# Four fp32 loads at the start of a Jensen-Shannon kernel, each split by partition halves over both hardware DMA queues, with p ahead of q

## The chip, the cores and the metric

The kernel runs on one core of one Trainium2 chip. The metric is device time in microseconds (us) of that core; lower is better. Times quoted are medians of several executions. Some executions fall in a slower state, over 1.5% above the fastest of the same kernel; they are called slow and the others fast. A ratio is the mean time of one kernel's fast runs over that of the other's of the same rounds, so it is not quite the ratio of the medians that stand beside it. The profiled execution has a *span* some 1.8 us shorter than its time, because the span leaves out what lies around the program.

## The reference

```python
batch, dim = 1024, 4096          # p and q: positive fp32 rows that sum to 1
m = 0.5 * (p + q)
kl_pm = np.sum(p * np.log(p / (m + 1e-8) + 1e-8), axis=-1)
kl_qm = np.sum(q * np.log(q / (m + 1e-8) + 1e-8), axis=-1)
return (0.5 * (kl_pm + kl_qm)).astype(np.float32)
```

## The kernel before

The rows lie eight to a partition, and the kernel walks through eight groups of 128 rows in blocks of columns. For each block it needs log p, log q and the log of the sum, all made by ScalarE (ACT). The first two blocks (512 and 256 columns, called block 0 and block 1 here) are loaded as fp32 by the hardware queues of SyncE (SP) and ScalarE. All others are loaded by GpSimd's queue, which casts to fp16 on the way; the third block (832 columns) is the first of these.

```python
for i in range(HW):                                   # HW = 2: blocks 0 and 1, fp32
    g, c0, w = loads[i]
    nc.sync.dma_start(out=early[i][:, 0, :], in_=pv[g, :, c0 : c0 + w])
    nc.scalar.dma_start(out=early[i][:, 1, :], in_=qv[g, :, c0 : c0 + w])
warm = small.tile([P, 1], fp32, tag="warm")
nc.vector.memset(warm, 1.0)
nc.scalar.activation(out=warm, in_=warm, func=Act.Ln)  # brings the table in
# ...
cast_loads(loads[HW : HW + 1])                        # third block, by GpSimd, with a cast
ident = small.tile([P, P], fp16, tag="ident")
make_identity(nc, ident)
# ...
cast_loads(loads[HW + 1 :])                           # all the rest
```

The order of work on ScalarE begins so (p, q: log of a block of p or q; c: log of a block's sum, which VectorE adds for blocks 0 and 1 and TensorE for all others):

```
p0 q0 c0 p1 q1 c1 p2 q2 c2 c3 p3 q3 c4 c5 ...
```

Of the kernel before, what the change touches and what calls it, by code (L numbers as in the profile page):

```python
# [91 lines left out]
def kernel(  # L92
# [6 lines left out]
    nc = tc.nc  # L99
    P = nc.NUM_PARTITIONS  # L100
# [13 lines left out]
    pv = p.rearrange("(p g) d -> g p d", g=n_rg)  # L114
    qv = q.rearrange("(p g) d -> g p d", g=n_rg)
# [35 lines left out]
    early = []  # L151
# [16 lines left out]

    for i in range(HW):
        g, c0, w = loads[i]  # L170
        nc.sync.dma_start(out=early[i][:, 0, :], in_=pv[g, :, c0 : c0 + w])
        nc.scalar.dma_start(out=early[i][:, 1, :], in_=qv[g, :, c0 : c0 + w])
    warm = small.tile([P, 1], fp32, tag="warm")
    nc.vector.memset(warm, 1.0)
    nc.scalar.activation(out=warm, in_=warm, func=Act.Ln)  # L175
    def cast_loads(some):
# [15 lines left out]
        out=half, in0=ident, scalar1=0.5, scalar2=0.0, op0=Alu.mult, op1=Alu.add  # L192
# [3 lines left out]
        out=less, in0=ident, scalar1=-0.5, scalar2=0.0, op0=Alu.mult, op1=Alu.add  # L196
# [242 lines left out]
    while any(queues):  # L439
        moved = False  # L440
        for todo in queues:
            while todo and all(d in emitted for d in after(*todo[0])):
                kind, i = todo.pop(0)
# [57 lines left out]
```

## Time and profile before

| | before |
|---|---|
| time, median of 6 runs | 98.19 us (97.82 to 98.51) |
| span of the profiled run | 96.0 us |
| ACT busy | 89.8 us, 94% of the span |
| ScalarE's first log, last log's end | 4.17 us, 92.25 us |

When each early load lands: the list of DMA issues of the kernel before, for the first 3.3 us, gives it. Its columns are: what is loaded, the queue that issues, count, size (for the casting loads in fp16), and us from the start of the issue to the landing.

```profile
t<-in_q_dram ACTq DMA_DIRECT2D x1, 256.0 KB, 3.6
t<-in_p_dram SPq DMA_DIRECT2D x1, 256.0 KB, 3.4
...
t<-in_p_dram POOLq DMA_DIRECT2D x1, 208.0 KB, 4.7
t<-in_q_dram POOLq DMA_DIRECT2D x1, 208.0 KB, 5.7
t<-in_q_dram ACTq DMA_DIRECT2D x1, 128.0 KB, 3.8
t<-in_p_dram SPq DMA_DIRECT2D x1, 128.0 KB, 3.4
```

With issues that start at 0.74 and 1.17 us, all four fp32 loads are there by 4.9 us. The casting loads of the third block are issued from 1.24 and 1.90 and land at 5.9 and 7.6.

### The profile page before, as it was taken

The numbers are of one execution on the slowest core, as the hardware profiler recorded it, in microseconds if no ns is written. First come the engines' busy times: TensorE is split into PE (matmuls) and PEld (weight loads), VectorE is DVE, ScalarE is ACT, GpSimd is POOL, SyncE is SP. The second block draws the span as 40 slices with busy tenths as digits, with TensorE's granted clock in tenths as the row PEclk, the third lists the DMA queues.
The fourth block names the chain that finished last, engine by engine and source line by source line (L and its number), as shares of the span: only waits on it lengthen the run. The fifth ranks groups of instructions, "written<-read, shape, count | busy, mean of one in ns | idle before, by whom it ended". The sixth has DMA issues, their size and how long they took to land.

```text
span 96.0 us, 1311 instructions
## 1 busy us (share of the span) xinstructions
PE 70.7 (74%) x468; PEld 45.3 (47%) x468; DVE 81.7 (85%) x87; ACT 89.8 (94%) x74; POOL 29.3 (31%) x60
## 2 busy tenths in 40 slices
PE   0799774886686678696785974984977989897740
PEld 0576441653465244463452642752552766656520
DVE  1378869999966988998979989979999999999990
ACT  3599999999999999999999999999999999999960
POOL 5974466443232424242313423335400000000000
PEclk9999999999999999999999999999999999999999
DMA  2999999999999999999999999999999999500000
GB/s 46 328 184 199 206 204 207 209 208 218 210 207 214 208 210 214 212 213 210 220 206 209 219 208 209 212 204 216 211 204 221 213 212 215 101 0 3 0 0 2
DMA packets 8502, 17.25 MB, mean 180 GB/s; under 512 B 1072, under 2 KB 3888, under 8 KB 8496
## 3 DMA queue, kind: packets, MB, share of 16 engines
q0 software_dynamic: 7776, 16.39, 90.1%
q1 hardware_dynamic: 432, 0.40, 1.5%
q10 hardware_dynamic: 288, 0.39, 1.2%
q8 instruction: 3, 0.05, 0.2%
q14 instruction: 3, 0.02, 0.1%
HBM read 33.55 MB, written 0.00 MB: 350 GB/s over the span
## 4 chain that ended last, share of the span: by engine, by line
ACT 43%; DMA 24%; issue 24%; DVE 2%; POOL 2%; PE 1%; ACTq 0%; POOLq 0%
ACT ab_t L281 25%; DMA t<-in_q_dram 24%; ACT c_t L299 17%; DVE c_t L343 1%; PE acc_t L360 1%; POOL t L179 1%; DVE ab_t L328 1%; POOL t L180 1%; ACT unused L371 0%; POOL ident masks.py:199 0%; POOL ident masks.py:197 0%; ACTq L299 0%; DVE res L376 0%; ACTq L496 0%; ACTq L281 0%
## 5 line engine op out<-in xcount | busy, mean ns | idle before, releaser
L281 ACT ACTIVATE ab_t<-t 128x2816 f16<-128x2816 f16 (+15 forms) x38 | 62.6, 1685 | 1.1 <-DMA t<-in_p_dram 1.0
L265 PE MATMUL st<-t,ident 128*128 128x512 f16 (+4 forms) x144 | 34.1, 352 | 7.4 <-DMA t<-in_q_dram 6.4
L311 DVE TENSOR_TENSOR ab_t<-ab_t,c_t 128x2816 f16<-128x2816 f16 (+12 forms) x25 | 29.3, 1180 | 6.7 <-ACT c_t L299 5.9
L360 PEld LDWEIGHTS <-half 128*128 128x128 f16 x268 | 25.4, 97 | 20.2 <-issue 16.3
L299 ACT ACTIVATE c_t<-st 128x1408 f16<-128x1408 f32 (+13 forms) x30 | 32.3, 1099 | 0.1
L360 PE MATMUL acc_t<-t,half 128*128 128x256 f16 (+2 forms) x200 | 23.9, 264 | 9.3 <-DVE t L321 9.0
L321 DVE TENSOR_TENSOR t<-t,ab_t 128x2816 f16<-128x2816 f16 (+11 forms) x23 | 28.2, 1234 | 1.2
L265 PEld LDWEIGHTS <-ident 128*128 128x128 f16 x144 | 13.6, 98 | 22.0 <-issue 11.7
L179 POOL DMA_DIRECT2D t<-in_p_dram x27 | 14.5, 536 | 20.4 <-DMA t<-in_p_dram 19.5
L180 POOL DMA_DIRECT2D t<-in_q_dram x27 | 14.4, 532 | 19.4 <-DMA t<-in_q_dram 19.3
L360 PE MATMUL acc_t<-ab_t,half 128*128 128x256 f16 x68 | 8.8, 270 | 2.4 <-DVE ab_t L328 2.4
L328 DVE TENSOR_TENSOR ab_t<-t,ab_t 128x1536 f16<-128x1536 f16 (+5 forms) x8 | 9.3, 1172 | 0.1
L253 PE MATMUL acc_t<-ones,ident 128*128 128x256 f16 x22 | 4.9, 420 | 3.1 <-POOL ident masks.py:199 3.1
L253 PEld LDWEIGHTS <-ident 128*128 128x128 f16 x22 | 3.2, 148 | 4.3 <-POOL ident masks.py:199 3.1
L339 DVE TENSOR_TENSOR c_t<-st,c_t 128x256 f16<-128x256 f32 (+2 forms) x3 | 3.7, 1217 | 0.0
L343 DVE CUSTOM_DVE_ANT_0 c_t<-st,c_t,run 128x1408 f16<-128x1408 f32 (+1 forms) x2 | 3.1, 1548 | 0.0
L343 DVE CUSTOM_DVE_ANT_0 c_t<-st,c_t 128x1024 f16<-128x1024 f32 (+1 forms) x2 | 3.0, 1484 | 0.0
L253 PE MATMUL acc_t<-ones,zero 128*128 128x256 f16 x22 | 2.9, 272 | 0.0
L175 ACT ACT_TABLE_LOAD x1 | 1.3, 1283 | 1.7 <-PEq L485 1.7
L382 DVE TENSOR_REDUCE res<-acc_t 128x1 f32<-128x256 f32 x6 | 2.5, 417 | 0.0
L253 PEld LDWEIGHTS <-zero 128*128 128x128 f16 x22 | 2.1, 98 | 0.2
L321 DVE TENSOR_TENSOR ab_t<-t,ab_t 128x1024 f16<-128x1024 f32 (+1 forms) x2 | 1.9, 958 | 0.1
(24 smaller groups left out, 9.7 us busy)
## 6 DMA issues: line engine op xcount, KB each, us to landing
t<-in_p_dram POOLq DMA_DIRECT2D x5, 352.0 KB, 12.4
t<-in_q_dram POOLq DMA_DIRECT2D x5, 352.0 KB, 12.8
t<-in_p_dram POOLq DMA_DIRECT2D x4, 384.0 KB, 11.8
t<-in_q_dram POOLq DMA_DIRECT2D x4, 384.0 KB, 12.0
t<-in_p_dram POOLq DMA_DIRECT2D x4, 320.0 KB, 12.7
t<-in_q_dram POOLq DMA_DIRECT2D x4, 320.0 KB, 12.8
t<-in_p_dram POOLq DMA_DIRECT2D x2, 512.0 KB, 13.3
t<-in_q_dram POOLq DMA_DIRECT2D x2, 512.0 KB, 14.5
```

Of the source, the lines that this page charges most:

```text
L179: nc.gpsimd.dma_start(out=v[:, 0, :], in_=pv[g, :, c0 : c0 + w])
L180: nc.gpsimd.dma_start(out=v[:, 1, :], in_=qv[g, :, c0 : c0 + w])
L253: nc.tensor.matmul(out=acc[g][:, :AW], lhsT=weights, rhs=ones, start=alone, stop=alone)
L265: nc.tensor.matmul(out=st[:, b : b + m], lhsT=ident, rhs=v[:, t, b : b + m], start=t == 0, stop=t == 1,)
L281: nc.scalar.activation(out=ab[k][:, which, o : o + w], in_=pq(g, c0, w)[:, which, :], func=Act.Ln, bias=TINY, scale=SHIFT,)
L299: nc.scalar.activation(out=c_t[:, :w], in_=s[j], func=Act.Ln, bias=SHIFT * 1e-8, scale=SHIFT * 0.5)
L311: nc.vector.tensor_tensor(out=v, in0=v, in1=c[j].unsqueeze(1).to_broadcast([P, 2, parts[j][2]]), op=Alu.subtract,)
L321: nc.vector.tensor_tensor(out=into, in0=u, in1=v, op=Alu.mult)
L328: nc.vector.tensor_tensor(out=ab[k], in0=u, in1=ab[k], op=Alu.mult)
L339: nc.vector.tensor_tensor(out=c[j], in0=s[j], in1=c[j], op=Alu.mult)
L343: nc.vector.tensor_tensor_reduce(out=c[j], in0=s[j], in1=c[j], scale=-0.5, scalar=before, op0=Alu.mult, op1=Alu.add, accum_out=now,)
L360: nc.tensor.matmul(out=acc[g][:, :m], lhsT=less if kind == "S" else half, rhs=v[:, t, b : b + m], start=(kind, i) == adds[g][0] and n == 0 ...
```

## The change

ScalarE waits 1.01 us for the first block of p. The change lets both queues fetch p first, half of the partitions each, and q after it, so that p is there sooner.

```diff
     for i in range(HW):
         g, c0, w = loads[i]
-        nc.sync.dma_start(out=early[i][:, 0, :], in_=pv[g, :, c0 : c0 + w])
-        nc.scalar.dma_start(out=early[i][:, 1, :], in_=qv[g, :, c0 : c0 + w])
+
+        for t, v in ((0, pv), (1, qv)):
+            for h, queue in ((0, nc.sync), (P // 2, nc.scalar)):
+                queue.dma_start(
+                    out=early[i][h : h + P // 2, t, :], in_=v[g, h : h + P // 2, c0 : c0 + w]
+                )
```

## The prediction

> **What bounds the kernel now.** I read the page first: the share of each engine, then the row of slices for ScalarE (ACT) and for the DMA engines.
>
> ```profile
> PE 70.7 (74%) x468; PEld 45.3 (47%) x468; DVE 81.7 (85%) x87; ACT 89.8 (94%) x74; POOL 29.3 (31%) x60
> ...
> ACT  3599999999999999999999999999999999999960
> ...
> DMA  2999999999999999999999999999999999500000
> ```
>
> Two things are near their limit together. ACT has 89.8 us of work in a span of 96.0 us, and the DMA engines are full from the second slice (2.4 us each) to the 34th, about 82 us. The change touches only the opening, so the question is what the opening is worth. The timeline of ACT shows it (start, duration, what, and in brackets the idle time before it):
>
> ```profile
> 0.74 0.89 ACTq L172 DMA_DIRECT2D t<-in_q_dram  x2
> 1.65 1.28 ACT L175 ACT_TABLE_LOAD   x1 [1.65 <-PEq L485]
> 2.95 0.20 ACT L175 ACTIVATE warm<-warm 128x1 f32<-128x1 f32 x1
> 4.17 1.15 ACT L281 ACTIVATE ab_t<-t 128x512 f16<-128x512 f32 x2 [1.01 <-DMA t<-in_p_dram]
> 5.22 0.61 ACT L299 ACTIVATE c_t<-s 128x512 f16<-128x512 f32 x1
> 5.74 0.71 ACT L281 ACTIVATE ab_t<-t 128x256 f16<-128x256 f32 x2
> 6.35 0.40 ACT L299 ACTIVATE c_t<-s 128x256 f16<-128x256 f32 x1
> 6.66 1.82 ACT L281 ACTIVATE ab_t<-t 128x832 f16<-128x832 f16 x2
> 8.58 0.93 ACT L299 ACTIVATE c_t<-st 128x448 f16<-128x448 f32 x2
> ```
>
> The second queue's two issues stand ahead of the table load, the table is ready at 3.15, and ACT then sits 1.01 us until the first block of p lands. That second of idle is what the change aims at. But whether ACT keeps what it wins depends on the next place where it waits for data. The same engine in narrow windows (start:end, length, busy, count, clock, DMA share, GB/s), asked because ACT's busy time between 7 and 9 us is 0.14 us short of full:
>
> ```profile
> 7.25:7.50 0.25, 0.25 (x1) 1.00 1.08 200
> 7.50:7.75 0.25, 0.21 (x2) 1.00 1.01 177
> ...
> 8.25:8.50 0.25, 0.23 (x1) 1.00 1.10 200
> 8.50:8.75 0.25, 0.17 (x1) 1.00 1.17 190
> ...
> 27.25:27.50 0.25, 0.19 (x1) 1.00 0.98 192
> 27.50:27.75 0.25, 0.22 (x1) 1.00 0.99 192
> ```
>
> ACT has three small gaps after its start: 0.04 us near 7.55 (before the log of the third q block, which starts at 7.58), 0.10 us before 8.58 (the log of that block's sum) and 0.09 us at 27.5. From there to its last log at 92.25 it has none. The chain of waits (start, length, what) says what the last of these gaps is:
>
> ```profile
> 3.51 6.41 DMA t<-in_q_dram
> 9.92 0.28 issue
> 10.20 7.02 DMA t<-in_q_dram
> 17.22 0.28 issue
> 17.51 9.94 DMA t<-in_q_dram
> ...
> 27.53 0.04 ACT ab_t L281
> ```
>
> So the end of the kernel is set by the stream of casting loads up to 27.45, by ACT from 27.53 to 92.25, and by a fixed tail of 3.75 us. ACT's opening is not on that path: ACT arrives at 27.5 with 0.09 us in hand.
>
> **What the Trainium skill says.** "DMA: Bandwidth & Descriptors", section "Rules for kernel authors", on two transfers to disjoint partition halves: "Don't bother — they serialize", because both halves spray over all 16 DMA engines. The same page, "Issuing engines are not separate DMA queues": issuing from several engines saves only sequencer time. The trace agrees so far: between 2.5 and 4.0 us the two hardware queues, each with whole blocks, together move 324 to 379 GB/s at a DMA share of 0.94 to 1.07, and no engine stands idle for the other queue. "Perfetto Trace Analysis", section "DMA Instruction — HWDGE (DVE, Sync)": the recorded issue includes the wait for a descriptor generator that the two sequencers share, and none of the data movement. Here the four issues took 377 to 459 ns, while data took 3.4 to 3.8 us to land. "ScalarE: Activation LUTs", "What ACT_TABLE_LOAD costs": 1283 ns; the trace has 1283 ns too. The page adds some 1380 ns of drain; this trace does not show it, the warm-up starts 0.02 us after the load.
>
> **The change, part by part.**
> 1. *Issues.* Each queue now issues four transfers of half the partitions where it issued two. On ACT two took 0.89 us. If the cost is per instruction, four take about 1.75 us, the table load moves from 1.65 to 2.5, ends at 3.8, and the warm-up at 4.0. If it is per descriptor, nothing moves and the table is ready at 3.15. I take the dearer: 3.9 to 4.0 (the next activation can start some 0.1 us before the recorded end of the one ahead, as 5.22 stands against 4.70 + 0.61).
> 2. *p0 lands earlier.* By the windows of 0.25 us, the hardware queues have moved about 39, 80, 147, 221, 309 and 399 KB by 2.0, 2.25, 2.5, 2.75, 3.0 and 3.25 us. Before, p0 shared this with q0: its 128 packets were through at about 3.45 and it was used at 4.17, so 0.7 us from last byte to first use. Now p0's 262 KB are first on both queues: through at 2.87, usable at about 3.6. The table load, not p0, then sets the start: 3.95, which is 0.2 us earlier than 4.17.
> 3. *q0 lands when it did.* p0 and q0 together are 524 KB, through at 3.6 in either order, so q0 is usable at about 4.3, against 4.37 (when VectorE began to add). The add took 692 ns, so the sum is ready at 5.0 to 5.05. The log of q0 follows p0's without a wait (3.95 + 0.53 = 4.48), and the log of the sum starts at about 5.05 in place of 5.22. What is left of the gain here is 0.15 to 0.2 us.
> 4. *It is given back at 7.58.* ACT would then finish the third p block at about 7.35 and need the third q block, which is loaded by the casting queue. That landed 5.7 us after an issue at 1.90, thus about 7.55. Its landing comes after all the hardware loads (786 KB), and the DMA engines have been full since 2 us: the order in which the hardware bytes go doesn't change when they are all done. So ACT's gap of 0.04 us becomes about 0.2 us, and the log of q2 starts at 7.58 as before.
> 5. *Beyond.* PE, VectorE and the pool issues see the same landings. Even if something were left, the gap at 27.5 would grow by it. Four more DMA instructions and perhaps a few extra semaphore waits of 17 to 21 ns are on no path that sets the end.
>
> Sum: start about -0.2, absorbed +0.2, at the end 0.0 us. A move of the casting stream itself, from a different packing of the first 786 KB, could shift everything by about 0.1 us either way.
>
> **The rivals.**
> *A: the gain is kept.* If the third q block landed earlier too, the whole path would come forward by up to 0.2 us, 98.1 us. For it: the DMA engines move only 160 GB/s in their first half microsecond, and two queues with work from the first moment may fill that better. Against it: the share there is already near 0.9, and ACT has only 0.09 us in hand at 27.5, so the stream alone can give at most some 0.1 us before ACT's own backlog from 8.58 binds. Both have to move together.
> *B: the issues cost more than the early p0 gives.* If the halves contend for the shared generator and take, say, 0.6 us each, ACT is through with issuing at 3.1, the table is ready at 4.6 and ACT starts 0.4 us late. The first two gaps take 0.14 us of it and the third 0.09, leaving 0.2 us: 98.5 us. For it: the second queue's data began about 0.25 us behind the first's though both issues began at 0.74. Against it: two issues on each side together already took only 0.89 us.
> *C: half-partition transfers run slower* because their spread over engines and memory ports is different. If 786 KB went at three quarters of the rate, the stream would lose some 0.7 us: 99.0 us. Nothing in this trace speaks for it; there is no 64-partition transfer in it.
>
> **Range and chances.** The best guess is the time before less a few hundredths: 98.3 us. Runs of the kernel before scatter from 98.04 to 98.47, which is more than A or half of B would move. 97.9 to 98.8 covers A with the scatter, B, and most of a mild C. A move of 2% is 1.97 us; nothing in the opening is that large, since the whole wait for p0 is 1.01 us and the loads are only 0.8 MB of 33.55 MB. I give 0.01 to faster, 0.98 to within 2%, and 0.01 to slower.
>
> **What would show the steps right or wrong.** Right: eight issues before 2.6 us and the table load at about 2.5 (step 1); the first log near 3.95, with its wait put down to nothing or to little of p (step 2); VectorE's first add at 4.3 to 4.4 (step 3); a gap on ACT of about 0.2 us just before 7.58 (step 4); and a log at about 27.5 that still waits for a q load. Step 1 falls if the table load stays near 1.65: then issues cost by descriptor and the first log starts near 3.6, but step 4 would still swallow it. Step 4 falls if the log of q2 starts more than 0.15 us earlier; then the casting stream moved, which would make A. The prediction is wrong altogether if the stream's landings move by more than half a microsecond, which would show as a lower DMA share or rate between 2 and 5 us.

## The result, and the profile after

The changed kernel takes 102.04 us (101.4 to 103.11, 6 runs, one of them slow; 101.79 without that one) against 98.19. The ratio of fast runs is 1.038, with a 95% interval of 1.0332 to 1.0428: **3.8% slower**, outside the predicted range of 97.9 to 98.8 us. The span grew from 96.0 to 100.0 us.

From the page of the changed kernel, engine shares and slices (2.5 us each):

```profile
PE 68.5 (68%) x468; PEld 45.5 (45%) x468; DVE 81.6 (82%) x87; ACT 89.9 (90%) x74; POOL 29.3 (29%) x60
...
ACT  0563999999999999999999999999999999999950
...
DMA  1999999999999999999999999999999993000000
```

ACT has the same work, 89.9 us, and the DMA engines are full from the second slice as before. Only ACT's first, third and fourth slices are clearly emptier. So nearly all of the loss lies in the first 10 us. The packet records agree: counted from the first packet of the loads, 7.79 MB had been read after 20 us in the kernel before, and 7.76 MB in the changed one. That first packet moves at 2.07 us instead of 1.75, and the stream stays 0.3 to 0.5 us behind; that is small beside what follows. What differs much is its order.

The timeline of ACT and of its queue in the changed kernel, against the one in the prediction:

```profile
0.74 0.57 ACTq L174 DMA_DIRECT2D t<-in_p_dram  x1
1.33 0.86 ACTq L174 DMA_DIRECT2D t<-in_q_dram  x1
2.22 0.62 ACTq L174 DMA_DIRECT2D t<-in_p_dram  x1
2.87 0.62 ACTq L174 DMA_DIRECT2D t<-in_q_dram  x1
3.52 1.28 ACT L179 ACT_TABLE_LOAD   x1 [3.52 <-issue]
...
4.92 0.61 ACT L285 ACTIVATE ab_t<-t 128x512 f16<-128x512 f32 x1
6.15 0.63 ACT L285 ACTIVATE ab_t<-t 128x512 f16<-128x512 f32 x1 [0.62 <-DMA t<-in_q_dram]
7.05 0.63 ACT L303 ACTIVATE c_t<-s 128x512 f16<-128x512 f32 x1 [0.27 <-DVE s L244]
7.59 0.40 ACT L285 ACTIVATE ab_t<-t 128x256 f16<-128x256 f32 x1
9.49 0.42 ACT L285 ACTIVATE ab_t<-t 128x256 f16<-128x256 f32 x1 [1.50 <-DMA t<-in_q_dram]
10.12 0.42 ACT L303 ACTIVATE c_t<-s 128x256 f16<-128x256 f32 x1 [0.21 <-DVE s L244]
```

Each issue of a half takes 0.57 to 0.86 us on ScalarE's queue (0.55 to 0.60 on SyncE's), where a whole load took 0.38 to 0.46. ACT is through with issuing at 3.49 us, not 1.62. The first log starts 0.75 us late. Then ACT waits for q0, for its sum, 1.50 us for q1 and for that sum. c1 starts at 10.12 us where it stood at 6.35 before: 3.77 us late.

The account up to the end of the last log (95.81 against 92.25 us, from ACT's timeline): 0.75 (start) + 0.62 + 0.27 + 1.50 + 0.21 (these waits) + 0.23 (one more, for TensorE, at 17 us) - 0.23 (the three gaps of the kernel before) + 0.2 (the remainder, not traced further) = 3.55 us.

A further 0.44 us comes after the output is issued: 2.76 us to the end of the span against 2.32. The traces show where. The output lands 1.41 us after its issue starts in both. SyncE closes the program with a list of semaphore checks, about 0.06 us each. In the kernel before, the output's check is the last: 0.08 us from landing to the end of the list. In the changed kernel the output is the ninth transfer of the hardware queues and shares the semaphore of the first; its check comes early, and seven others stand behind it: 0.51 us. The other profiles with exactly eight hardware loads show the same 0.51 us, experiment 1's whole loads included; with six loads (block 0 alone in halves) it is 0.08. This part of the loss has nothing to do with late loads.

TensorE's granted clock also differs: 1.00 throughout in the kernel before, 0.83 between 10 and 20 us in the changed one, and 0.66 to 0.83 there in the other late runs of the table at the end of the experiments. It does not carry the loss. ScalarE's only wait for TensorE is the 0.23 us above, and from the start of c1 to the end of the last log it takes 85.69 us against 85.90. Why the clock fell was not tested.

When the loads of the changed kernel land is in its list of issues for the first 3.3 us (columns as above):

```profile
t<-in_p_dram POOLq DMA_DIRECT2D x1, 208.0 KB, 4.0
t<-in_q_dram POOLq DMA_DIRECT2D x1, 208.0 KB, 5.4
...
t<-in_q_dram ACTq DMA_DIRECT2D x1, 128.0 KB, 4.8
t<-in_q_dram SPq DMA_DIRECT2D x1, 128.0 KB, 4.6
...
t<-in_q_dram SPq DMA_DIRECT2D x1, 64.0 KB, 5.9
t<-in_q_dram ACTq DMA_DIRECT2D x1, 64.0 KB, 6.6
```

The third block's casting loads land *sooner* than before (4.0 and 5.4 us after their issue instead of 4.7 and 5.7), and the halves of q later. Put in order of time, with the end of each issue and the landing, from the completion records of the two traces:

| kernel before: issue ends | lands | changed kernel: issue ends | lands |
|---|---|---|---|
| p0, q0: 1.12, 1.13 | 4.14, 4.34 | p0 halves: 1.29, 1.31 | 3.40, 3.92 |
| p1, q1: 1.60, 1.62 | 4.59, 4.91 | **third block's p: 1.90** | **5.26** |
| **third block's p: 1.90** | **5.90** | q0 halves: 1.92, 2.19 | 5.96, 6.13 |
| **third block's q: 2.43** | **7.56** | **third block's q: 2.43** | **7.29** |
| | | p1 halves: 2.56, 2.84 | 6.97, 7.49 |
| | | q1 halves: 3.20, 3.49 | 8.51, 9.46 |

In both kernels loads land about in the order in which their issues end. Before, all four fp32 loads were issued ahead of the casting loads. Now only p0 is. The casting load that was issued at 1.90 moved its first packet after 4.0 us in the kernel before, and between 2.75 and 3.0 us in the changed one: as far as the traces tell it was ready that early in both, but in the first the loads of the hardware queues were ahead of it.

This gave the theory that the experiments test, called **Late** in the expectations: the halves come late because there are more issues and longer ones, so casting loads overtake q0, p1 and q1, and ScalarE, which takes its work in order, waits. The rivals are **Half** (transfers of 64 partitions are slow in themselves), **Table** (only the later table load counts) and **Order** (p ahead of q is what hurts).

### The profile page after: what moved, and what is told of

The parts are those of the page before. It is cut to its first block, busy times and chain, and to the rows that moved or that the text cites. A ratio compares the mean times of both kernels' runs of the same rounds, so it can differ in the third digit from the quotient of the medians.

```text
span 100.0 us, 1324 instructions
## 1 busy us (share of the span) xinstructions
PE 68.5 (68%) x468; PEld 45.5 (45%) x468; DVE 81.6 (82%) x87; ACT 89.9 (90%) x74; POOL 29.3 (29%) x60
## 4 chain that ended last, share of the span: by engine, by line
ACT 47%; issue 22%; DVE 3%; PE 1%; ACTq 0%
ACT ab_t L285 24%; ACT c_t L303 23%; DVE c_t L347 1%; PE acc_t L364 1%; DVE t L325 1%; DVE ab_t L332 1%; ACT unused L375 0%; DVE res L386 0%; ACTq L303 0%; DVE res L380 0%; ACTq L500 0%; ACTq L285 0%; DVE run L347 0%
## 5 line engine op out<-in xcount | busy, mean ns | idle before, releaser
L285 ACT ACTIVATE ab_t<-t 128x2816 f16<-128x2816 f16 (+15 forms) x38 | 63.6, 1718 | 2.1 <-DMA t<-in_q_dram 2.1
L364 PE MATMUL acc_t<-t,half 128*128 128x256 f16 (+2 forms) x200 | 24.4, 270 | 16.7 <-DVE t L325 16.6
L303 ACT ACTIVATE c_t<-st 128x1408 f16<-128x1408 f32 (+13 forms) x30 | 33.2, 1135 | 0.2 <-PE st L269 0.2
L269 PE MATMUL st<-t,ident 128*128 128x512 f16 (+4 forms) x144 | 31.8, 357 | 1.0 <-DVE c_t L343 0.8
L257 PE MATMUL acc_t<-ones,ident 128*128 128x256 f16 x22 | 4.0, 362 | 3.1 <-POOL ident masks.py:199 3.1
L244 DVE TENSOR_TENSOR s<-t 128x512 f32<-128x512 f32 (+1 forms) x2 | 1.1, 558 | 5.6 <-DMA t<-in_q_dram 5.6
L179 ACT ACT_TABLE_LOAD x1 | 1.3, 1283 | 3.5 <-issue 3.5
```

The lines of the kernel that those rows point to most:

```text
L257: nc.tensor.matmul(out=acc[g][:, :AW], lhsT=weights, rhs=ones, start=alone, stop=alone)
L269: nc.tensor.matmul(out=st[:, b : b + m], lhsT=ident, rhs=v[:, t, b : b + m], start=t == 0, stop=t == 1,)
L285: nc.scalar.activation(out=ab[k][:, which, o : o + w], in_=pq(g, c0, w)[:, which, :], func=Act.Ln, bias=TINY, scale=SHIFT,)
L303: nc.scalar.activation(out=c_t[:, :w], in_=s[j], func=Act.Ln, bias=SHIFT * 1e-8, scale=SHIFT * 0.5)
L364: nc.tensor.matmul(out=acc[g][:, :m], lhsT=less if kind == "S" else half, rhs=v[:, t, b : b + m], start=(kind, i) == adds[g][0] and n == 0 ...
```

## The experiments

### 1. Late issues without halves

```diff
 # the kernel before, inside the loop, after the loads of block 0
+        if i == 0:
+            for k in range(2):
+                tiny = small.tile([P, 2, 8], fp32, tag=f"tiny{k}")
+                nc.sync.dma_start(out=tiny[: P // 2, 0, :], in_=pv[g, : P // 2, :8])
+                nc.scalar.dma_start(out=tiny[: P // 2, 1, :], in_=qv[g, : P // 2, :8])
```

> The kernel before, with two transfers of 32 bytes a row (64 partitions) on each hardware queue between the first and the second block: no halved load, but the issues of p1 and q1 end at about 2.8 us instead of 1.6. Theory Late (the DMA engines serve the transfers about in the order in which their issues end, so hardware loads issued after the casting loads of p2 and q2, whose issues end at 1.90 and 2.44, land behind them): q1 lands at 7.5 to 8 us instead of 5.0, ScalarE waits for it, and the time is 99.5 to 100.5 us. Rival Half (transfers of 64 partitions move slowly in themselves): no change, 98.2 us. Rival Table (what costs is only the activation table, loaded 1.2 us later): the first log starts at 4.3 instead of 4.17, 98.3 us.

Measured: 100.85 us, ratio 1.0285 (1.0244 to 1.0326). The issue of q1 ended at 3.25 us, it landed at 8.81, and ScalarE waited 2.34 us for block 1. The loss is a little above the expected one (0.43 us of it is the end of the program, see above), with both blocks whole and no small piece but four transfers of 2 KB. ScalarE's line for p1 and q1:

```profile
8.67 0.72 ACT L286 ACTIVATE ab_t<-t 128x256 f16<-128x256 f32 x2 [2.34 <-DMA t<-in_p_dram]
```

A late issue is enough; Half and Table are not needed for it.

### 2. The table load ahead of ScalarE's issues

```diff
 # the kernel before
+    warm = small.tile([P, 1], fp32, tag="warm")
+    nc.vector.memset(warm, 1.0)
+    nc.scalar.activation(out=warm, in_=warm, func=Act.Ln)
     for i in range(HW):
         ...
-    warm = ...      # the three lines that stood here
```

> The kernel before, with the table load and the warm-up ahead of ScalarE's two DMA issues, so that q0 and q1 are issued from about 2.3 to 3.2 us, whole. Late: q0's issue ends after those of both casting loads of the third block, so it lands at 6.5 to 7.5 us instead of 4.35 and ScalarE waits for it; 100.5 to 102 us, with no half-transfer anywhere. Half: 98.2 to 98.6 us. Table: the table is there earlier, so no loss at all, 98.0 us.

Measured: 98.13 us, ratio 1.0012 (0.9955 to 1.0069). The expectation failed, since the edit did not do what I thought. ACT's timeline in this run:

```profile
0.74 1.28 ACT L171 ACT_TABLE_LOAD   x1 [0.74 <-PEq L485]
...
0.91 0.86 ACTq L175 DMA_DIRECT2D t<-in_q_dram  x2
...
3.49 0.63 ACT L281 ACTIVATE ab_t<-t 128x512 f16<-128x512 f32 x1 [1.26 <-DMA t<-in_p_dram]
4.42 0.63 ACT L281 ACTIVATE ab_t<-t 128x512 f16<-128x512 f32 x1 [0.30 <-DMA t<-in_q_dram]
```

The issues start at 0.91, *beside* the table load, and end at 1.77, still ahead of the casting load's 1.90. So nothing came late, and nothing was lost. The run shows something else: p0 lands early here, at 3.47, and ScalarE's first log starts 0.68 us earlier than in the kernel before, with no gain at the end. But this is not yet step 4 of the prediction: the early start is gone by c0, which starts at 5.22 as before, because ScalarE waits 0.30 us for q0 and 0.17 us for its sum. (The third block's p landed late in this run, at 7.15, and cost a wait of 0.40 us.)

### 3. Casting loads held back, three pairs

A pair is the changed kernel and the kernel before with the same edit. The first pair:

```diff
+    pad = small.tile([P, P], fp16, tag="pad")
+    for _ in range(10):
+        nc.gpsimd.memset(pad, 0.0)
     cast_loads(loads[HW : HW + 1])
```

> The changed kernel, with ten GpSimd memsets of 128x128 ahead of the first casting load, so that all casting loads are issued after about 3.6 us, behind all eight halves. Late: the eight halves land in one run, q1 by about 5.3 us instead of 9.5; ScalarE then waits for the held casting loads, and the time is that of the kernel before with the same ten memsets, within 0.7 us. Half: the halves are still slow, q1 lands after 7 us, and the kernel is over 2 us slower than the kernel before with the memsets.

> The kernel before with the same ten memsets, as the control. Casting loads are issued from about 3.6 us instead of 1.24; their data began only at 4.0 us in the kernel before, so the stream is about 0.7 to 1.2 us later, and the time is 98.8 to 99.5 us. Both theories say the same here; it is the time that the changed kernel with memsets is to be held against.

Measured: 101.12 us (ratio 1.0297, 1.0245 to 1.035) and 99.16 us (1.0117, 1.0069 to 1.0165). The pair is 2 us apart, against Late's 0.7. But the edit missed: the first casting load was issued from 3.25 us, while the last half's issue ran until 3.49, and that half landed at 7.39 where all the others were there by 5.89. The pair decides nothing. The second pair had twenty memsets, and the table load first:

> The changed kernel with the activation table loaded ahead of ScalarE's DMA issues (the kernel before lost nothing by that) and twenty memsets ahead of the casting loads, so that these are issued from about 5.3 us on, well behind the last half (about 3.7) and, by the first such pair, with most halves landed. Late: the halves land undisturbed by 5.5 us, nothing is left of the loss, and the time is that of the kernel before with the same two edits within 0.4 us. Half (transfers of 64 partitions are slow, or leave the DMA engines uneven for long): 1 us or more slower than that kernel, as the pair with ten memsets was 2 us apart.

> The control: the kernel before with the table load first and twenty memsets. The casting stream begins about 2 us later than with ten memsets, after the hardware loads have ended, so that its delay passes to the end: 100.2 to 101.5 us by both theories.

Measured: 102.53 us (1.0453, 1.0412 to 1.0495) and 102.56 us (1.0439, 1.0369 to 1.0509): equal. But both had a wait of my own making: VectorE stood behind the identity matrix, which came after the memsets, and ScalarE waited for VectorE's sum until 8.6 us in both. In the third pair the identity is built first:

```diff
-    cast_loads(loads[HW : HW + 1])
     ident = small.tile([P, P], fp16, tag="ident")
     make_identity(nc, ident)
+    pad = small.tile([P, P], fp16, tag="pad")
+    for _ in range(17):
+        nc.gpsimd.memset(pad, 0.0)
+    cast_loads(loads[HW : HW + 1])
```

> The pair with twenty memsets was muddied: VectorE waited for the identity matrix behind the memsets, in both kernels. Here the identity is built first, then seventeen memsets, then the casting loads, from about 5.2 us; table load first, loads in halves as in the changed kernel. Late: the halves meet no casting load, q1 lands by 5.7 us, ScalarE is through with both blocks and waits for the third, and the time equals that of the kernel before with the same edits within 0.4 us. Half: at least 1 us slower than that kernel.

> The control for it: the kernel before with whole loads, the table load first, the identity first, seventeen memsets, then the casting loads. The casting stream starts over 2 us later than in the kernel before: 100.5 to 102.5 us by both theories.

Measured: 102.25 us (1.0385, 1.0305 to 1.0465; the ratio leaves one slow run out) and 101.36 us (1.0353, 1.0263 to 1.0442). The means of the fast runs, 101.96 and 101.60 us, differ by 0.36 us with wide intervals, which is just within the 0.4 us that Late allows and far from the 3.8% of the change. The landings say it more sharply. The last half of q1 landed at 5.92 us, 2.43 us after its issue ended; the whole q1 of the control landed at 4.87, 3.10 us after. ScalarE then waits for the third block in both; the changed kernel first, then the control:

```profile
9.36 1.88 ACT L288 ACTIVATE ab_t<-t 128x832 f16<-128x832 f16 x2 [1.79 <-DMA t<-in_p_dram]
```

```profile
9.43 1.88 ACT L284 ACTIVATE ab_t<-t 128x832 f16<-128x832 f16 x2 [2.84 <-DMA t<-in_p_dram]
```

Both start the third block at about the same time, when the same casting load has landed. Half falls: with no casting load in the way the halves land promptly and leave no trace at this point. (The two profiled spans are 100.7 and 99.7 us. Of the difference, 0.42 us is the list of checks at the end; the other 0.6 us are longer waits for casting loads after 12 us, 1.5 against 0.95 us in all, one of 1.34 us at 29 us among them. Why these are longer was not tested.)

### 4. Which part of the change: order, shape or count

p's halves on the one queue and q's on the other, so that p is not ahead of q:

```diff
-        for t, v in ((0, pv), (1, qv)):
-            for h, queue in ((0, nc.sync), (P // 2, nc.scalar)):
+        for h in (0, P // 2):
+            for t, v, queue in ((0, pv, nc.sync), (1, qv, nc.scalar)):
```

> The changed kernel with its eight halves, but p's four on the one hardware queue and q's four on the other, as the whole loads stood before: halving without 'p ahead of q'. Late (a hardware load whose issue ends after a casting load's issue lands behind it; issues of a half take 0.55 to 0.86 us): the issues end at the same times as in the changed kernel, so q0 lands near 6 us and q1 near 9 us, and the time is within 0.7 us of the changed kernel's 102.0. Rival Order (p ahead of q on both queues is what hurts, not the halving): about 98.2 us. Rival Half: near 102 as well.

Measured: 101.78 us, 1.0403 (1.0346 to 1.0459). q0 landed at 6.59, q1 at 9.13. Order falls.

Halves by columns, all 128 partitions in each:

```diff
-            for h, queue in ((0, nc.sync), (P // 2, nc.scalar)):
+            for b, queue in ((0, nc.sync), (w // 2, nc.scalar)):
                 queue.dma_start(
-                    out=early[i][h : h + P // 2, t, :], in_=v[g, h : h + P // 2, c0 : c0 + w]
+                    out=early[i][:, t, b : b + w // 2], in_=v[g, :, c0 + b : c0 + b + w // 2]
                 )
```

> Each of the four loads in two halves again, p ahead of q, but halved by columns: 128 partitions in every transfer, eight issues as in the changed kernel. If an issue of 128 partitions costs 0.38 to 0.46 us whatever its count, q0's issues end at 1.65 us, ahead of the first casting load's (1.90), and q1's at 2.5, about with the second's (2.44): Late says q0 lands at 4.4, q1 at 7 to 8, time 99 to 100.5 us. If each takes 0.57 as the halves do, Late says as the changed kernel, 102 us. Rival Half (64 partitions are slow as such): 98.3 us.

Measured: 101.52 us, but with two of four runs slow; the two fast ones took 100.78 and 100.49, too few for an interval. Issues took 0.38 to 0.46 us each and ended at 2.58. q0's ended at 1.59 and 1.62, ahead of the casting load's 1.90, and it landed at 4.48 and 4.74. p1's (2.07 and 2.10) landed at 7.15 and 7.36, between the third block's p (6.34) and q (7.90); q1's at 8.11 and 8.31, after both. So the count alone costs much of it: c1 starts at 8.96 us, 2.61 us late where it was 3.77 us in the changed kernel. The rest goes with the longer issues of 64 partitions. Half falls once more, as no transfer here had 64.

All eight halves on one queue:

```diff
-            for h, queue in ((0, nc.sync), (P // 2, nc.scalar)):
+            for h, queue in ((0, nc.sync), (P // 2, nc.sync)):
```

> All eight halves on the sync queue, p ahead of q. ScalarE issues nothing, so its table is there at about 2.2 us. With 0.57 us an issue the last ends at about 5.4 us. Late: q0's issues end at 3.1 us, behind both casting loads of the third block, so it lands at 7 to 8 us, q1 at 11 or later, and the time is 103 to 105.5 us, slower than the changed kernel. Rival Table (the table load behind four issues is the main cost): faster than the changed kernel, 99 to 100.5 us.

Measured: 104.02 us, 1.0646 (1.0581 to 1.0711). The issues, 0.53 to 0.65 us each without any other hardware queue beside them, ended at 5.81 us; q0 landed at 8.16 and q1 at 11.86. The table was loaded at 0.73. Table falls as the main cost, and Late's size was right.

Only block 0 in halves, block 1 whole:

> Only the first block's p and q are halved over both queues; the second block is loaded whole, p1 by one queue and q1 by the other: three issues each. Late: q0 as in the changed kernel (issues end at 1.9 and 2.2, lands near 6 us), p1 and q1 end at about 2.5 and 2.85, just behind the second casting load, and land at 7.5 to 8.5 instead of 7.5 and 9.5: 100.3 to 101.4 us. Half: half of the loss would be left or less, 99.5 to 100 us.

Measured: 99.90 us, 1.021 (1.0149 to 1.0271), a little better than expected. p1 and q1 landed at 7.94 and 8.15, q0 at 6.59.

The changed kernel with the table load first (the edit of experiment 2):

> The changed kernel with the table load and the warm-up ahead of ScalarE's DMA issues; the issues run beside the table load, as the kernel before with that edit showed. The first log starts at about 4.0 us instead of 4.92, but q0 still lands at 6.1 or a little later and q1 near 9.5. Late: no gain, 101.7 to 102.3 us. Table: 101.1 us or less.

Measured: 100.89 us, 1.0318 (1.0246 to 1.0389), about 0.6% below the change's 1.038, with intervals that overlap. It was run at another time. By the numbers this is what Table had forecast (101.1 or less), not Late. The trace speaks against Table all the same: the first log started at 4.13, 0.79 us earlier, but ScalarE waited 1.74 us for q0 afterwards and started c0 at 7.27, later than the changed kernel's 7.05. The gain came after that, with q1, which landed at 8.87 instead of 9.46, so that c1 started 0.67 us earlier. So the early table itself gave nothing here; whether it helped q1 land earlier is not told apart from scatter.

### 5. Is it ScalarE's wait for block 1 that costs?

The loads of the changed kernel are left as they are; only the order of work is altered, the third block ahead of block 1. ScalarE's order becomes `p0 q0 c0 p2 q2 c2 c3 p1 q1 c1 p3`, and VectorE's and TensorE's follow.

> The changed kernel with nothing altered in its loads; only the order of work: the third block (the first cast one), whose loads land at 5.2 and 7.3 us, is taken ahead of the second, whose q half lands at 9.5. Late, with the loss made by engines that wait in order for late hardware loads: ScalarE reaches the fourth block's log at about 11.1 us instead of 12.8 and the time falls by 1.4 to 1.9 us, to 100.1 to 100.6. If something else than the wait for the second block makes the loss (a slower stream of loads): no change, 102 us.

Measured: 102.04 us, 1.0413 (1.0353 to 1.0472), no change. This looked like a blow to Late, but the trace showed that I had put VectorE's sum of block 1 behind the products of the third block, and ScalarE waited 1.51 us for that sum at 12.70 us. Mended:

```diff
-a0 u0 x0 u2 u3 x2 x3 a1 u1 x1 u4
+a0 u0 x0 a1 u2 u3 x2 x3 u1 x1 u4
```

> Again the changed kernel with its loads untouched and the third block's work ahead of the second's. In the first form VectorE's sum of the second block stood behind the third block's products, and ScalarE waited 1.5 us for it; now that sum stands ahead of them. Late: ScalarE has the third block's logs to do while q1 is on its way, reaches the fourth block at 11.2 to 11.6 us instead of 12.8, and the time falls to 100.4 to 101.0 us. If the loss is not made by ScalarE waiting in order for the second block: 102 us.

Measured: 99.97 us (99.49 to 100.84), 1.0162 (1.009 to 1.0234). More than half of the loss is gone, a little more than expected, without touching a load. ScalarE reached the fourth block at 11.75 us (12.81 in the changed kernel, 9.39 before); the time fell by more than the 1.06 us of the profiled run, which was the slowest of the four (they scatter by 1.35 us). What remains is mainly the wait for q0, 1.50 us here, the late start, a wait of 0.38 us for TensorE and the list of checks at the end.

### 6. How exact is the order?

```diff
 # the changed kernel
+    pad = small.tile([P, P], fp16, tag="pad")
+    for _ in range(3):
+        nc.gpsimd.memset(pad, 0.0)
     cast_loads(loads[HW : HW + 1])
```

> The changed kernel with three memsets (0.6 us) ahead of the casting loads. In the changed kernel the first casting load's issue ended at 1.90 us, q0's halves' at 1.92 and 2.19; now it ends at about 2.5 and the second's at 3.04. Late in its exact form (service in the order in which issues end): q0 lands at 4.6 to 5.0 us instead of 6.1, ahead of the third block's p; q1's halves (3.2 and 3.5) are still behind both casting loads and land at 8.5 to 9.5, so the time stays at 101.3 to 102.3 us. If the hardware queues merely get a small share beside the casting queue: q0 moves little.

Measured: 101.91 us, 1.0383 (1.0322 to 1.0444), the time as expected but not the landing. Three memsets held the casting load back by 0.17 us, not 0.6: its issue ran from 1.41 to 2.07, between the ends of q0's two halves (1.92 and 2.19). q0 landed at 6.69 and 6.86, ahead of the casting load (7.25), but not early. The two moved at the same time. So "in order of issue" is only rough: loads issued within some tenths of a microsecond of each other share the engines. In the run with all halves on one queue, both halves of p1 even landed ahead of casting loads whose issues had ended 0.3 and 0.5 us before theirs (9.14 against 9.31 us, 10.38 against 10.70).

### 7. What an issue costs

Eighteen transfers on the idle sync queue of the kernel before, three each with 128, 64, 128, 32, 96 and 128 partitions and 512 bytes a row.

> The kernel before with eighteen transfers of 512 bytes a row added to the otherwise idle sync queue, three each with 128, 64, 128, 32, 96 and 128 partitions in turn: the cost of an issue by itself (the time of the kernel means nothing here). If the partition count makes it: 128 takes 0.38 to 0.46 us, 64 takes 0.55 to 0.60, the first 128 after a 64 about 0.59 as in two earlier runs, and later ones 0.4 again. If instead everything issued while other queues are busy takes 0.58, all but the first would.

One run (101.22 us). The issues took, in turn: 128 partitions 0.43, 0.43, 0.70; 64: 0.53, 0.47, 0.64; 128: 0.66, 0.43, 0.43; 32: 0.34, 0.32, 0.31; 96: 0.31, 0.31, 0.31; 128: 0.35, 0.35, 0.43. A group of 64 is dearer than most of 128, but 96 is the cheapest, and single issues of 128 go to 0.70. This does not confirm a rule by partition count, and what makes an issue long stays open. That the halves' issues were long stands from eleven profiles: 0.53 to 0.87 us in every one, against 0.36 to 0.46 for the same loads whole or cut by columns. But whole loads were long too where they followed transfers of 64 partitions: 0.58 to 0.60 us for p1 and q1 in experiment 1 and with only block 0 in halves.

### 8. Can the early start be kept?

```diff
 # the kernel before, table load first; columns of the blocks of the first group
-[512, 256, 832, 960, 768, 768]
+[512, 256, 640, 1152, 768, 768]
```

(The products' and sums' blocks follow.)

> An attempt to use what the runs showed: the kernel before with the table load first (the first log then starts at 3.5 us) and 192 columns moved from the third block to the fourth, so that the third's q, for which ScalarE waited in both kernels, lands about 0.5 us earlier. If ScalarE's wait there is what swallowed the earlier start: 97.5 to 97.9 us, 0.2 to 0.5% faster than the kernel before. If the stream to 27.5 us binds regardless: 98.0 us.

Measured: 98.08 us, 0.9987 (0.9935 to 1.004): the same. ScalarE no longer waits for the third block, but the early start is gone before that, as in experiment 2 (c0 starts at 5.24), and ScalarE waits 0.42 us for a casting load at 24.97. No version beats the kernel before.

### The sum of it

Ten profiled runs leave the order of work and the start of the casting loads as they were. For nine of them, the start of c1, the last ScalarE work that needs an fp32 load, against the span of the same run:

| run | c1 starts | span | span less c1 |
|---|---|---|---|
| before | 6.35 | 96.0 | 89.65 |
| before, table first | 6.37 | 96.5 | 90.13 |
| only block 0 in halves | 8.65 | 98.1 | 89.45 |
| halves by columns | 8.96 | 99.0 | 90.04 |
| tiny transfers, no halves | 9.29 | 99.1 | 89.81 |
| changed, table first | 9.45 | 99.1 | 89.65 |
| halves, own queues | 9.78 | 99.8 | 90.02 |
| changed | 10.12 | 100.0 | 89.88 |
| all on one queue | 12.44 | 102.3 | 89.86 |

c1 moves by 6.1 us and the last column stays within 0.7. Whatever makes c1 late makes the end late by nearly as much: ACT has hardly a gap after it. (The six rows with eight hardware loads hold 0.43 us of checks at the end that the others don't.) The tenth run, experiment 7, shows another way to lose: c1 starts at 6.54 us there, but the span is 99.5, because with the eighteen transfers in progress ScalarE waited for casting loads at four places, 2.6 us in all.

## Why the prediction was wrong

- **Step 1, the issues: mis-sized.** It put ACT's four issues at 1.75 us and the table load at 2.5 us. They took 2.75 us, and the table load came at 3.52. The term that was off is the cost of an issue: 0.44 us assumed, 0.57 to 0.86 measured.
- **Step 2, p0 earlier: right in its direction, too large.** The halves of p0 landed at 3.40 and 3.92 us; ScalarE needs both, and whole p0 had landed at 4.14. So 0.22 us were won, where "usable at about 3.6" against 4.17 promised nearly 0.6. The longer issues delayed the first packet from 1.75 to 2.07 us, and p0's last packet ended at 3.26, not 2.87. (One reading was off too: before, p0's 2 KB packets ended at 3.72, not 3.45, because p1's packets had already begun among them.)
- **Step 3, "q0 lands when it did": this step failed.** Predicted 4.3 us, measured 6.13. The working added up hardware bytes and took it that they all stay ahead of the casting stream. That held before only because all four fp32 loads were issued by 1.62 us, ahead of the casting load's 1.90. In the changed kernel the issues of q0's halves end at 1.92 and 2.19. What the runs showed in its place: a casting load overtakes a hardware load that is issued after it, and ScalarE waits for the overtaken load, 0.62 us for q0 and 1.50 us for q1. Experiment 1 shows the overtaking without halved data, and the third pair of experiment 3 shows the halves without the overtaking.
- **Step 4, "given back at 7.58": right in its principle, but not met here.** A gain at the start is swallowed: experiment 2 began 0.68 us earlier and ended at 1.0012, though there q0 swallowed it and not the third block. The sentence that rested on the same bytes, that the order of the hardware bytes does not change when they are all done, was wrong: q1 came at 9.46 us instead of 4.91, after the q of the third block.
- **Step 5, nothing beyond: wrong for a delay.** With 0.09 us in hand at 27.5 us I concluded that the opening is not on the path. The slack was small, so the opening was off the path for gains only. A delay of 3.77 us at c1 passed to the end nearly whole (3.55 us at the last log's end). For the same reason the argument for 0.98 to "within 2%" fails: the wait of 1.01 us for p0 limits what the opening can gain, not what it can lose. And the "extra semaphore waits" that were to be on no path cost 0.43 us at the end of the program.
- **Rivals.** B had the right cause for a loss, issues of 0.6 us, and made 98.5 us of it, because it counted only the later table and not what the later loads would meet. (The second queue's data began 0.19 us behind the first's, 1.94 against 1.75, not 0.25.) C, slow half-transfers, is ruled out as a main cause by the third pair and by the halves by columns. A did not happen.

Open stay: what makes an issue of 64 partitions long, and the exact rule by which the DMA engines share themselves between queues.

## What to carry to other kernels

Splitting a load buys its early landing with more issues, and issues on a queue come one after another: work out when the *last* of them ends, and what other queues will have issued by then. Loads that are needed first have to be issued first across all queues: here q1, issued behind two casting loads, landed 4.55 us later than before. And a chain with little slack is one-sided: here it swallowed a gain at its start and passed on a delay nearly in full.

## What the Trainium skill lacked or had wrong

- "DMA: Bandwidth & Descriptors", "Queues, rings and completion order", says each DMA engine round-robins by packet between the queues that have work. Here a casting load, issued by 1.90 us, moved nothing until 4.0 us while loads issued earlier by the hardware queues were in progress, though it could begin before 3.0 us in the changed kernel. Loads landed about in the order in which their issues ended; only loads issued within some tenths of a microsecond of each other visibly shared (experiment 6). When the casting load's descriptors reached the engines is not in the records.
- The same page, "Rules for kernel authors", advises against two transfers of disjoint partition halves because they serialize. It is right that nothing is gained at the end. It lacks the price: eight half issues ended at 3.49 us instead of four whole ones at 1.62, which let other loads overtake and made most of the 3.8% here.
- The same page, "Issuing engines are not separate DMA queues", calls the issue time "usually small relative to the DMA itself". Here 0.55 to 0.86 us an issue, for data that took 2.7 to 6.6 us to land, decided the time. No page that I read gives the cost of a hardware-queue issue by shape on this chip: 0.36 to 0.46 us for whole loads with no transfer of 64 partitions ahead of them, 0.53 to 0.87 for halves by partition.
- "ScalarE: Activation LUTs", "What ACT_TABLE_LOAD costs": the load's 1283 ns agree. The 1380 ns of drain, which the page gives for a switch to another set, were not seen at this first load of the program (the warm-up starts 0.02 us after it), and the section lacks that ScalarE's DMA issues can run beside a table load (issues from 0.91 to 1.77 us, table load from 0.74 to 2.02).
- No page that I read has the cost of each of the semaphore checks that close a program: about 0.06 us here, and 0.51 instead of 0.08 us from the output's landing to the end of the list with eight hardware loads.
